# Turning keys, values and normed outputs of the prompt off TensorE: 32x32 blocks on VectorE and a round trip through DRAM, with the projections in another order

## The chip, the cores and the metric

One core of a Trainium2 chip runs the whole kernel. The metric is the device time of one execution in microseconds; of the kernel before it is the median of three runs, 1311.06 us.

## The reference, cut to what matters

One layer of a hybrid decoder over 1024 prompt tokens and 64 sample tokens (8 sequences of 8), model width 1024, all in float32. A combined projection gives queries, keys, values and gates for four retention heads and four mLSTM heads of width 128. Each head runs chunk by chunk (128 tokens), here for retention:

```python
def step(S, inp):
    qc, kc, vc = inp
    scores = jnp.einsum('bhnd,bhmd->bhnm', qc, kc) * dmat[None]
    out = (jnp.einsum('bhnm,bhmv->bhnv', scores, vc)
           + jnp.einsum('bhnd,bhdv->bhnv', qc, S) * xi[None, :, :, None])
    S_new = (S * chunk_decay[None, :, None, None]
             + jnp.einsum('bhmd,bhmv->bhdv', kc * zeta[None, :, :, None], vc))
    return S_new, out
...
ret_y = head_groupnorm(ret_out, ret_g) * jax.nn.silu(g_r)
...
ml_y = head_groupnorm(ml_out, ml_g) * jax.nn.sigmoid(o_m)
mix = jnp.concatenate([ret_y, ml_y], axis=-1).astype(x.dtype) @ w_out
```

The mLSTM heads do the same with data-dependent weights and a normaliser. After the mix come a residual, and a feed-forward layer with a short convolution. The state update contracts over tokens, the scores over the head's width, and the output projection over the width again; so keys and values are needed with features on the partitions and with tokens on the partitions, and the normed output has to be turned back.

## The kernel before, in words

Activations lie with features on the 128 partitions and tokens along the free axis, T = 1088 of them (1024 prompt, 64 sample), in four blocks b of 272 columns. `proj` computes one 128-wide piece of a projection: for each block `dense` issues 24 products (8 slices of the contraction, three terms of a split into high and low parts, line 160), 96 per projection; then an evacuation writes the block to a tile of tag `tok` (five of them): `evac_copy` by ScalarE for values, `evac_rot` (rotary) or `evac_norm` by VectorE for queries and keys. Two weight pieces are staged ahead by SP (`stage_w`, line 132) and split by ScalarE (line 144) and VectorE (line 146). `psA` has two PSUM banks, `psB` six.

`mix_head` runs for four retention heads (r0 to r3) and four mLSTM heads (m0 to m3). It projects queries, keys, values in this order (values of r0 and r1 come at the very start, as a pair). Then it goes through the chunks in pairs, [0,1] to [6,7], and the sample chunk [8]. `front` turns keys and values of a pair by TensorE into the PSUM bank `x_` (lines 632 and 633; `ident` is the identity), from which VectorE makes `kz` (keys times decay, line 636 or 640) and ScalarE `vt` (values times the norm of the token, line 644), computes the scores (line 666) and weighs them into `pt`. `pair_of` computes the state update (line 774) and the output (lines 779 and 781), evacuates the output to an `on` tile (three of them) and takes its statistics. `finish`, once for chunks 0 to 3, once for 4 to 7 and once for the sample, normalises `on` (line 707), turns it by TensorE (line 710) and scales it into the output tile `yT` (line 716 by VectorE for retention heads, where `yT` holds the gate already; line 718 by ScalarE for mLSTM heads). `finish` is held back: `finish_previous(b, row)` calls it within the next head's projections, with its transposes behind block b's products and its first VectorE operation behind an evacuation.

Order within an engine is set by a scheduler that simulates a timeline; `tc.issue_after` adds edges by hand. So the next head's first projection fills TensorE between the products of a head's chunks. Meanwhile GpSimd computes sums of feed-forward weights (`weight_sums`, line 823), a background stream of loads, subtractions and stores, first in the tile `wq`, later in `tab`, where the rotary tables were. They are read back in the feed-forward layer.

Of the kernel before, what the change touches and what calls it, by code (L numbers as in the profile page):

```python
# [16 lines left out]
P = 128  # L17
# [75 lines left out]
def hybrid_layer_kernel(ctx: ExitStack, tc: tile.TileContext, a: dict, o: dict):  # L93
# [166 lines left out]
    def tok(name, rows=P, dt=F32):  # L260
        return tokp.tile([P, T], dt, tag="tok", name=name)[:rows, :]
# [26 lines left out]
    wv = [tuple(wp.tile([P, D], F32R, tag="w" + part, name=f"w{part[0]}_in{i}") for part in ("hi", "lo")) for i in first]  # L288
    split_piece = lambda n, *after: split_to(*(t[:, pieces[n]] for t in (staged[0], *wv[0])), nc.vector, *after)
    split_piece(0)  # L290
    sums = [m2.tile([P, NB, 129], F32, tag=t, bufs=1, name=f"sums_{t}").rearrange("p s v -> p (s v)") for t in ("vx", "sb")]
    sqs = [tok(f"sq{i}").rearrange("p (k n) -> p k n", k=4) for i in range(2)]
    for b in range(5):
        if b % 2 == 0 and b < 4:
            h.append(quadrants("h", b // 2))
        if b < 4:
            gain_split(xs[b], V_PREMIX, h[b // 2], b)
        if b == 0:
            split_to(staged[1], *wv[1])
            continue  # L300
        nts.append(sums[(b - 1) // 3][:, (b - 1) % 3 * Q:((b - 1) % 3 + 1) * Q])
        last["sums"] = square_sum(xs[b - 1], nts[-1], sqs, nc.gpsimd if b == 4 else nc.vector)
# [22 lines left out]
        return out  # L325

    def spread_tile(name):
        return m2.tile([P, NB * 129], F32, tag="vx", bufs=1, name=name)

    rbd = dr.tile([1, T], F32, name="rbd")  # L330

# [36 lines left out]
        nc.scalar.activation(ig, ig, AF.Identity, bias=vec[0:NH, V_BG + 1:V_BG + 2])  # L368

    def gate_consts():  # L370
        xst = m2.tile([P, X_N], F32, tag="vx", bufs=1, name="xst")
        nc.sync.dma_start(xst, a["cx"])
        nc.vector.tensor_copy(upb, xst[:, X_UP:X_UP + P])
        for t in vts:
            nc.gpsimd.memset(t[:, :, P:P + 1], 1.0)
        nc.vector.tensor_copy(negsb, xst[:, X_NEGS:X_NEGS + P])
# [82 lines left out]


    yT = []

    def proj(*jobs, mid=None, done=None, banks=lambda i, b: psA, pair=False):

# [91 lines left out]
    def mix_head(hd, ml):  # L556
# [3 lines left out]
        if hid == 0:  # L560
            vs = [tok(f"v_r{i}") for i in range(2)]
            proj(*((i, evac_copy(t), w) for i, t, w in zip(first, vs, wv)),
                 banks=alternate, pair=True)
            early.extend(vs)
        v = early.pop(0) if early else tok(f"v_{nm}")
        q, k = tok(f"q_{nm}"), tok(f"k_{nm}")
        if ml:
            ub = ub_tile(f"ub{hd}")
            row = urows[hd:hd + 1, :]
            nc.sync.dma_start(ub, bass.AP(row.tensor, row.offset, [[0, P], [1, UB]]))  # L570
            proj((16 + hd, evac_norm(q, 1.0), split_w(staged.pop(), f"in{16 + hd}")))
            row = last["row", 3]
            proj((20 + hd, evac_norm(k, SCALE)), banks=alternate)
            finish_previous(2, row)
            proj((24 + hd, evac_copy(v)))
            finish_previous(1, last["row", 3])
            finish_previous(2, last["row", 3])
        else:
            eq, ek = evac_rot(q, f"q{nm}"), evac_rot(k, f"k{nm}")
            if hd == 0:  # L580
                proj((0, eq, split_to(stage_w(a["wi"][0], "in0"), *first_q)), mid=pre_norm, banks=lambda i, b: psB)
                here["wq"] = mp.tile([P, 2, 2, 2 * P], F32, tag="wq", name="wq")
                proj((NH, ek))
            else:
                proj((hd, eq))
                row = last["row", 3]
                proj((NH + hd, ek), banks=alternate)
                finish_previous(2, row)
                if hd == 1:
                    finish_previous(3, last["row", 1])  # L590
                    finish_previous(3, last["row", 2])
            if hd == 0:
                token_norms()
            if hd > 1:
                proj((2 * NH + hd, evac_copy(v)))
                finish_previous(1, last["row", 3])
                finish_previous(2, last["row", 3])
            if hd == 0:
                gate_proj()
                gate_consts()  # L600
                for _ in range(5):
                    next(rows)
                for i in range(NH):
                    proj((12 + i, early_gate(i)), banks=alternate)
                    next(rows)
                    next(wsums)
                log_exp_tables(last["sigmoid"])
                next(rows)

        if hid >= NH - 1:  # L610
            j = 12 + hid + 1 if hid + 1 < 2 * NH else 28
            staged.append(stage_w(a["wi"][j], f"in{j}"))
        sb = m2.tile([P, NB, 129], F32, tag="sb", bufs=1, name=f"sb_{nm}")
        nc.sync.dma_start(sb[:, :, :P], a["sc" if ml else "sr"][hd].rearrange("p (s v) -> p s v", s=NB))
# [6 lines left out]
        def front(cs):  # L621

            c0, L = cs[0], len(cs)
            nmc = f"{nm}{c0}"
            px = bank(psB, 512, f"x_{nmc}").rearrange("p (j i n) -> p j i n", j=2, i=2)
            if c0 < 8:
                kc, vc = ([chunk(t, c) for c in cs] for t in (k, v))
            else:
                own.append(spread_tile(f"sp_{nm}"))
                kc, vc = ([spread_copy(t, own[0][:, i * P:(i + 1) * P])] for i, t in enumerate((k, v)))  # L630
            for i, c in enumerate(cs):
                nc.tensor.transpose(px[:, 0, i, :], kc[i], ident)
                nc.tensor.transpose(px[:, 1, i, :], vc[i], ident)
            kz = m2.tile([P, 2, P], F32, tag="kz", name=f"kz_{nmc}")
            if ml:
                nc.vector.tensor_tensor(kz[:, :L], px[:, 0, :L, :],
                                        cols[:, c0:c0 + L, NH + hd].unsqueeze(2).broadcast_to([P, L, P]), ALU.mult)
            else:
                zc = C_ZE + hd + (0 if c0 < 8 else NH)
                nc.vector.tensor_scalar(kz[:, :L], px[:, 0, :L, :], rc(zc, 1), None, ALU.mult)  # L640
            vt = vts[0]
            vts.append(vts.pop(0))
            for i, c in enumerate(cs):
                nc.scalar.activation(vt[:, i, :P], px[:, 1, i, :], AF.Copy, scale=rcol[:, c:c + 1])
            qs = None
            if ml:
                wt, qs = (here["wq"][:, turns["wq"] % 2, i].rearrange("p (i n) -> p i n", i=2) for i in range(2))
# [35 lines left out]
        def finish(on, mv, c0, L, name, after=None, row=None):  # L683

            sh = [P, L]
            small = lambda tag: m2.tile([P, 4], F32, tag=tag, name=f"{tag}_{name}")[:, :L]
            vv, A = small("vv"), small("A")
            if ml:
                den, rd = small("den"), small("rd")
                dd = on[:, :L, P]  # L690
                with tc.issue_after(row.ins) if row else nullcontext():
                    nc.vector.scalar_tensor_tensor(den, dd, -1.0, dd, ALU.mult, ALU.max)
# [12 lines left out]
            ps = bank(psB, L * P, f"yt_{name}")  # L705
            for i in range(L):
                nc.vector.scalar_tensor_tensor(on[:, i, :P], on[:, i, :P], mv[:, i, 0:1],
                                               A[:, i:i + 1].broadcast_to([P, P]), ALU.subtract, ALU.mult)
                with tc.issue_after(after.ins) if after else nullcontext():
                    nc.tensor.transpose(ps[:, i * P:(i + 1) * P], on[:, i, :P], ident)  # L710
            y = yT[hid // 2][:, hid % 2, c0 * CH:c0 * CH + L * P if c0 < 8 else T]
            if c0 == 8:
                ps, y = spread(ps)[:, :, LEAD:], spread(y)
            gain = vec[:, V_HEAD + hid:V_HEAD + hid + 1]
            if hid in EARLY:
                nc.vector.scalar_tensor_tensor(y, ps, gain, y, ALU.mult, ALU.mult)
            else:
                nc.scalar.activation(y, ps, AF.Copy, scale=gain)
# [837 lines left out]
```

## Time and profile before

| | |
|---|---|
| median of 3 runs | 1311.06 us (1310.99 to 1311.78) |
| profiled execution, its own time | 1311.53 us |
| its span | 1309.7 us |
| TensorE busy | 1296.0 us, 99%, 10501 products |
| VectorE, ScalarE, GpSimd busy | 998.3, 600.0, 430.8 us |
| heads: first scores of r0, first scores of m0, start of the output projection | 110.80, 291.81, 495.09 us |
| output projection, feed-forward layer | from 495.09 us to the end |
| transfers | 194.46 MB, 148 GB/s in the mean |

Spans of products overlap since products are pipelined; what one takes from TensorE is the distance between starts. A row of a group gives line, engine, operation, names of output and inputs, shapes and count, then busy time and mean duration in ns, then idle time before it. A row of one line or tile gives durations as minimum/median/maximum. Rows by stretch give busy time of each engine with the number of instructions, the granted clock of TensorE, the busy share of the 16 transfer engines and GB/s. A row of transfers gives size and time to landing; a row of a queue gives packets, MB and the share of 16 engines.

### The profile page before, as it was taken

How to read it: one execution, taken by the hardware profiler on the slowest of the kernel's cores; microseconds unless marked ns; L12 is line 12 of the kernel's file. 1: busy time of each engine (PE TensorE's matmuls, PEld its weight loads, DVE VectorE, ACT ScalarE, POOL GpSimd, SP SyncE). 2: the span in 40 equal slices, each digit the busy share in tenths (PEclk: the TensorE clock that was granted, in tenths of full speed). 3: DMA queues.
4: the chain of work that ended last, by engine and by line, in shares of the span. 5: the costliest groups of instructions: out<-in, count | busy, mean ns of one | idle time of the engine just before them, and what ended most of it. 6: DMA issues, size and time to landing. Idle time of an engine off the chain costs nothing.

```text
span 1309.7 us, 26782 instructions
## 1 busy us (share of the span) xinstructions
PE 1296.0 (99%) x10501; PEld 1285.9 (98%) x10501; DVE 998.3 (76%) x2002; ACT 600.0 (46%) x1144; POOL 430.8 (33%) x564
## 2 busy tenths in 40 slices
PE   9999999999999999999999999999999999999996
PEld 9999999999999999999999999999999999999996
DVE  7774766657767655678999878787787888897678
ACT  7544433323433346455744434343443455543563
POOL 0354341758882000001334321222222214593002
PEclk9999999999999999999999999999999999999998
DMA  7344443567783124233144433444334469533363
GB/s 262 109 139 150 148 147 116 181 193 236 239 267 123 51 66 152 69 103 134 53 153 163 150 120 120 149 138 144 115 125 156 132 207 311 175 95 95 95 222 137
DMA packets 90784, 194.46 MB, mean 148 GB/s; under 512 B 13849, under 2 KB 39065, under 8 KB 90146
## 3 DMA queue, kind: packets, MB, share of 16 engines
q1 hardware_dynamic: 78210, 150.30, 34.4%
q0 software_dynamic: 12160, 41.95, 9.7%
q8 instruction: 82, 1.34, 0.4%
q10 hardware_dynamic: 288, 0.50, 0.1%
q14 instruction: 44, 0.36, 0.1%
HBM read 136.21 MB, written 56.50 MB: 147 GB/s over the span
## 4 chain that ended last, share of the span: by engine, by line
PE 96%; DVE 2%; DMA 1%; ACT 1%; issue 0%; SPq 0%
PE in L160 30%; PE out L160 7%; PE up_S L1130 6%; PE up_S L1129 6%; PE up_S L1128 6%; PE dn L1355 5%; PE dn L1356 5%; PE dn L1357 5%; PE up_A L1129 5%; PE up_A L1128 5%; PE up_A L1130 5%; PE up_A L1180 1%; PE up_A L1179 1%; PE up_A L1178 1%; DVE facc L1432 1%; PE s_r L666 1%
## 5 line engine op out<-in xcount | busy, mean ns | idle before, releaser
L160 PE MATMUL in<-hh,wh_in 128*128 128x272 f32 x960 | 277.8, 292 | 0.8 <-ACT hh L227 0.8
L160 PE MATMUL in<-hh,wl_in 128*128 128x272 f32 x960 | 277.4, 291 | 0.2 <-DVE wl_in L146 0.2
L160 PE MATMUL in<-hl,wh_in 128*128 128x272 f32 x960 | 277.1, 291 | 0.0
L160 PEld LDWEIGHTS in<-hh,wh_in 128*128 128x128 f32 x960 | 180.1, 188 | 2.8 <-issue 1.4
L160 PEld LDWEIGHTS in<-hh,wl_in 128*128 128x128 f32 x960 | 180.3, 188 | 1.4 <-issue 1.0
L160 PEld LDWEIGHTS in<-hl,wh_in 128*128 128x128 f32 x960 | 179.8, 188 | 0.9 <-issue 0.7
L144 ACT ACTIVATE wh_up<-st_up 128x1024 fp32r<-128x1024 f32 x84 | 80.5, 960 | 168.8 <-PE up_S L1129 97.1
L146 DVE TENSOR_TENSOR wl_up<-st_up,wh_up 128x1024 fp32r<-128x1024 f32 x84 | 96.0, 1144 | 9.9 <-ACT wh_up L144 9.9
L1102 DVE TENSOR_TENSOR Uv<-Uv,up_S 128x272 f32<-128x272 f32 (+1 forms) x200 | 66.4, 374 | 45.5 <-PE up_S L1130 45.5
L1283 DVE TENSOR_TENSOR rb<-rb 128x544 fp32r<-128x544 f32 x78 | 75.6, 974 | 28.7 <-ACT rb L1282 28.1
L1304 POOL TENSOR_TENSOR wd<-wd 128x512 f32<-128x512 f32 x44 | 74.5, 1715 | 47.0 <-DMA wd<-in_wd 20.0
L1282 ACT ACTIVATE rb<-rb 128x544 fp32r<-128x544 f32 x78 | 50.7, 651 | 82.2 <-DMA rb<-bd 71.2
L823 POOL TENSOR_TENSOR tab<-tab 128x256 f32<-128x256 f32 x104 | 79.1, 771 | 11.9 <-DMA tab<-in_wu 7.4
L1163 POOL TENSOR_TENSOR act<-act 128x544 f32<-128x544 f32 x40 | 63.4, 1586 | 58.0 <-DMA bd<-act 36.2
L1093 POOL MEMSET Ug<- 128x2 f32 x22 | 2.2, 99 | 221.5 <-DMA xr<-in_x 100.2
L1143 DVE SCALAR_TENSOR_TENSOR c<-Uv,vec,c 128x1024 f32<-128x1024 f32 (+1 forms) x88 | 68.5, 783 | 8.5 <-ACT c L1141 8.5
L1143 DVE SCALAR_TENSOR_TENSOR c<-Ug,vec,c 128x1024 f32<-128x1024 f32 x88 | 69.1, 825 | 0.0
L823 POOL TENSOR_TENSOR wq<-wq 128x256 f32<-128x256 f32 x56 | 47.8, 863 | 45.8 <-DMA wq<-in_wu 43.6
L144 ACT ACTIVATE wh_in<-st_in 128x1024 fp32r<-128x1024 f32 (+2 forms) x31 | 31.9, 1028 | 57.0 <-PE in L160 56.1
L1141 ACT ACTIVATE c<-Ug,vec 128x1024 f32<-128x1024 f32 (+1 forms) x44 | 34.6, 834 | 45.5 <-DVE Ug L1106 43.9
L823 POOL DMA_DIRECT2D tab<-in_wu x52 | 36.8, 713 | 33.1 <-DVE k_r L500 21.7
L1130 PE MATMUL up_S<-T1h,wl_up 128*128 128x272 f32 x160 | 46.4, 290 | 0.0
(557 smaller groups left out, 4652.8 us busy)
## 6 DMA issues: line engine op xcount, KB each, us to landing
rb<-bd SPq DMA_DIRECT2D x76, 272.0 KB, 2.8
st_up<-sd SPq DMA_DIRECT2D x40, 512.0 KB, 3.9
bd<-act SPq DMA_DIRECT2D x33, 544.0 KB, 3.3
st_in<-in_wi SPq DMA_DIRECT2D x31, 512.0 KB, 3.8
tab<-in_wu POOLq DMA_DIRECT2D x52, 256.0 KB, 5.3
sd<-tab POOLq DMA_DIRECT2D x26, 512.0 KB, 3.6
st_up<-in_wu SPq DMA_DIRECT2D x24, 512.0 KB, 3.2
wd<-in_wd SPq DMA_DIRECT2D x44, 256.0 KB, 5.1
```

The source lines that it names most:

```text
L144: act = nc.scalar.activation(hi, x, AF.Copy)
L146: last["split"] = act, eng.tensor_tensor(lo, x, hi.bitcast(F32), ALU.subtract)
L160: last["product", b] = nc.tensor.matmul(ps, u[:, k * P:(k + 1) * P], x[b // 2][k // 4][v][:, k % 4, qcols(b)], start=k == term == 0, stop= ...
L823: last["sums"] = f(*args)
L1102: nc.vector.tensor_tensor(o_, o_ if x is None else c(x), c(ps), ALU.add)
L1128: nc.tensor.matmul(ps, wh[:, c], xh[:, k, n], start=k == 0, stop=False)
L1129: nc.tensor.matmul(ps, wh[:, c], xl[:, k, n], start=False, stop=False)
L1130: nc.tensor.matmul(ps, wl[:, c], xh[:, k, n], start=False, stop=k == 3)
L1143: last["conv"] = nc.vector.scalar_tensor_tensor(c, u(i), cw(i), c, ALU.mult, ALU.add)
L1283: nc.vector.tensor_tensor(lo, x, hi.bitcast(F32), ALU.subtract)
L1304: last[out] = nc.gpsimd.tensor_tensor(quad(p, out), quad(p, x), quad(p, y), op)
L1355: nc.tensor.matmul(t, wh[:, ms], ah, start=k == 0, stop=False)
```

## The change

For the prompt's eight chunks, TensorE no longer turns anything. `flip` takes a finished half of a projection (blocks 0 and 1, or 2 and 3: 512 columns), lets VectorE transpose its 32x32 blocks into the one tile of tag `flip`, which also orders the columns by block, and writes it to a tile in DRAM; after the second half four transfers read it back, each to 32 partitions, with runs of 128 elements. Values are read back into their own tile, keys into another (`kt`). `flip_rows` does the same for the normed output of four chunks. `flipped` is the view through which `kz`, `vt` and the final scale read. The sample chunk is turned by TensorE as before. Each `mix_head` projects keys, then values, then queries, and the held-back `finish` calls move with them: the first behind the values, the second behind the first block's row of the queries, the sample's behind the second. Retention heads get the gain by ScalarE in place and the gate by VectorE, instead of one VectorE operation. Two spread tiles (`sums_0`, and the tile of tag `vx`) change their place or size.

```diff
+    CH4 = 4 * P
+    def flip(dst, src, name):
+        bounce = dr.tile([2, P, CH4], F32, tag="bounce", bufs=4, name=f"bounce_{name}")
+        def f(b):
+            if b % 2 == 0:
+                return
+            d = m2.tile([P, CH4], F32, tag="flip", bufs=1, name=f"flip_{name}{b // 2}")
+            x = src[:, b // 2 * CH4:(b // 2 + 1) * CH4]
+            nc.vector.transpose(d.rearrange("p (j c b) -> p c j b", j=4, c=4), x.rearrange("p (c j a) -> p c j a", c=4, j=4))
+            nc.sync.dma_start(bounce[b // 2], d)
+            if b == 3:
+                rows_ = bounce.rearrange("h (i a) n -> a (h i) n", i=4)
+                for j in range(4):
+                    nc.sync.dma_start(dst[32 * j:32 * j + 32, :8 * P].rearrange("p (g n) -> p g n", g=8),
+                                      rows_[:, :, j * P:(j + 1) * P])
+        return f
+    def flip_rows(dst, x, name):
+        bounce = dr.tile([P, CH4], F32, tag="bounce_y", bufs=4, name=f"bounce_{name}")
+        d = m2.tile([P, CH4], F32, tag="flip", bufs=1, name=f"flip_{name}")
+        nc.vector.transpose(d.rearrange("p (j c b) -> p c j b", j=4, c=4), x)
+        nc.sync.dma_start(bounce, d)
+        rows_ = bounce.rearrange("(i a) n -> a i n", i=4)
+        for j in range(4):
+            nc.sync.dma_start(dst[32 * j:32 * j + 32].rearrange("p (g n) -> p g n", g=4), rows_[:, :, j * P:(j + 1) * P])
...
             proj(*((i, evac_copy(t), w) for i, t, w in zip(first, vs, wv)),
-                 banks=alternate, pair=True)
+                 banks=alternate, pair=True,
+                 done=lambda b, fs=[flip(t, t, f"v_r{i}") for i, t in enumerate(vs)]: [f(b) for f in fs])
...
+        kt = yT[hid // 2][:, hid % 2] if ml else ub_tile(f"kt_{nm}")
+        flip_k = flip(kt, k, f"k_{nm}")
         if ml:
...
-            proj((16 + hd, evac_norm(q, 1.0), split_w(staged.pop(), f"in{16 + hd}")))
+            proj((20 + hd, evac_norm(k, SCALE), split_w(staged.pop(), f"in{20 + hd}")), done=flip_k)
             row = last["row", 3]
-            proj((20 + hd, evac_norm(k, SCALE)), banks=alternate)
+            proj((24 + hd, evac_copy(v)), done=flip(v, v, f"v_{nm}"))
             finish_previous(2, row)
-            proj((24 + hd, evac_copy(v)))
-            finish_previous(1, last["row", 3])
-            finish_previous(2, last["row", 3])
+            proj((16 + hd, evac_norm(q, 1.0)), banks=alternate)
+            finish_previous(3, last["row", 0])
+            finish_previous(3, last["row", 1])
...
             if c0 < 8:
-                kc, vc = ([chunk(t, c) for c in cs] for t in (k, v))
+                kx, vx = flipped(kt, c0, L), flipped(v, c0, L)
+                kc = [chunk(k, c) for c in cs]
...
-            for i, c in enumerate(cs):
-                nc.tensor.transpose(px[:, 0, i, :], kc[i], ident)
-                nc.tensor.transpose(px[:, 1, i, :], vc[i], ident)
...
+                turned = on.rearrange("p i w -> p (i w)")[:, :CH4]
+                flip_rows(turned, on[:, :, :P].rearrange("p c (j a) -> p c j a", j=4), f"y_{name}")
+                ps, y = flipped(turned, 0, 4), y.rearrange("p (c i b) -> p c i b", c=4, i=4)
             gain = vec[:, V_HEAD + hid:V_HEAD + hid + 1]
-            if hid in EARLY:
+            if hid in EARLY and c0 < 8:
+                nc.scalar.activation(turned, turned, AF.Copy, scale=gain)
+                nc.vector.tensor_tensor(y, y, ps, ALU.mult)
+            elif hid in EARLY:
                 nc.vector.scalar_tensor_tensor(y, ps, gain, y, ALU.mult, ALU.mult)
             else:
                 nc.scalar.activation(y, ps, AF.Copy, scale=gain)
```

More of the change, by code (lines that the diff above doesn't have):

```diff
@@ L290, in hybrid_layer_kernel @@
     split_piece(0)
-    sums = [m2.tile([P, NB, 129], F32, tag=t, bufs=1, name=f"sums_{t}").rearrange("p s v -> p (s v)") for t in ("vx", "sb")]
     sqs = [tok(f"sq{i}").rearrange("p (k n) -> p k n", k=4) for i in range(2)]
+    sums = [tok("sums_0"), m2.tile([P, NB, 129], F32, tag="sb", bufs=1, name="sums_1").rearrange("p s v -> p (s v)")]
     for b in range(5):
@@ L327, in spread_tile @@
     def spread_tile(name):
-        return m2.tile([P, NB * 129], F32, tag="vx", bufs=1, name=name)
+        return m2.tile([P, 4 * 129], F32, tag="vx", bufs=1, name=name)
     rbd = dr.tile([1, T], F32, name="rbd")
@@ L370, in gate_consts @@
     def gate_consts():
-        xst = m2.tile([P, X_N], F32, tag="vx", bufs=1, name="xst")
+        xst = m2.tile([P, 4 * 129], F32, tag="vx", bufs=1, name="xst")[:, :X_N]
         nc.sync.dma_start(xst, a["cx"])
@@ L461, in hybrid_layer_kernel, with flipped @@
     yT = []
+    CH4 = 4 * P
[22 more added lines that the diff above has]
+            nc.sync.dma_start(dst[32 * j:32 * j + 32].rearrange("p (g n) -> p g n", g=4), rows_[:, :, j * P:(j + 1) * P])
+    def flipped(t, c, L):
+        c0 = c % 4
+        return t[:, c // 4 * CH4:(c // 4 + 1) * CH4].rearrange("p (i c b) -> p c i b", i=4, c=4)[:, c0:c0 + L]
     def proj(*jobs, mid=None, done=None, banks=lambda i, b: psA, pair=False):
@@ L582, in mix_head @@
                 here["wq"] = mp.tile([P, 2, 2, 2 * P], F32, tag="wq", name="wq")
-                proj((NH, ek))
+                proj((NH, ek), done=flip_k)
             else:
-                proj((hd, eq))
+                proj((NH + hd, ek), done=flip_k)
                 row = last["row", 3]
-                proj((NH + hd, ek), banks=alternate)
-                finish_previous(2, row)
                 if hd == 1:
+                    proj((hd, eq), banks=alternate)
+                    finish_previous(2, row)
+                    finish_previous(3, last["row", 0])
                     finish_previous(3, last["row", 1])
-                    finish_previous(3, last["row", 2])
             if hd == 0:
@@ L594, in mix_head @@
             if hd > 1:
-                proj((2 * NH + hd, evac_copy(v)))
-                finish_previous(1, last["row", 3])
-                finish_previous(2, last["row", 3])
+                proj((2 * NH + hd, evac_copy(v)), done=flip(v, v, f"v_{nm}"))
+                finish_previous(2, row)
+                proj((hd, eq), banks=alternate)
+                finish_previous(3, last["row", 0])
+                finish_previous(3, last["row", 1])
             if hd == 0:
@@ L610, in mix_head @@
         if hid >= NH - 1:
-            j = 12 + hid + 1 if hid + 1 < 2 * NH else 28
+            j = 16 + hid + 1 if hid + 1 < 2 * NH else 28
             staged.append(stage_w(a["wi"][j], f"in{j}"))
@@ L624, in front @@
             nmc = f"{nm}{c0}"
-            px = bank(psB, 512, f"x_{nmc}").rearrange("p (j i n) -> p j i n", j=2, i=2)
+            wide = lambda t: t.rearrange("p c (i b) -> p c i b", i=4)
             if c0 < 8:
-                kc, vc = ([chunk(t, c) for c in cs] for t in (k, v))
+                kx, vx = flipped(kt, c0, L), flipped(v, c0, L)
+                kc = [chunk(k, c) for c in cs]
             else:
@@ L630, in front @@
                 kc, vc = ([spread_copy(t, own[0][:, i * P:(i + 1) * P])] for i, t in enumerate((k, v)))
-            for i, c in enumerate(cs):
-                nc.tensor.transpose(px[:, 0, i, :], kc[i], ident)
-                nc.tensor.transpose(px[:, 1, i, :], vc[i], ident)
+                px = bank(psB, 2 * P, f"x_{nmc}").rearrange("p (j n) -> p j n", j=2)
+                nc.tensor.transpose(px[:, 0, :], kc[0], ident)
+                nc.tensor.transpose(px[:, 1, :], vc[0], ident)
+                kx, vx = (wide(px[:, i:i + 1, :]) for i in range(2))
             kz = m2.tile([P, 2, P], F32, tag="kz", name=f"kz_{nmc}")
             if ml:
-                nc.vector.tensor_tensor(kz[:, :L], px[:, 0, :L, :],
-                                        cols[:, c0:c0 + L, NH + hd].unsqueeze(2).broadcast_to([P, L, P]), ALU.mult)
+                nc.vector.tensor_tensor(wide(kz[:, :L]), kx, cols[:, c0:c0 + L, NH + hd].unsqueeze(2).unsqueeze(3)
+                                        .broadcast_to([P, L, 4, 32]), ALU.mult)
             else:
                 zc = C_ZE + hd + (0 if c0 < 8 else NH)
-                nc.vector.tensor_scalar(kz[:, :L], px[:, 0, :L, :], rc(zc, 1), None, ALU.mult)
+                nc.vector.tensor_scalar(wide(kz[:, :L]), kx, rc(zc, 1), None, ALU.mult)
             vt = vts[0]
@@ L643, in front @@
             for i, c in enumerate(cs):
-                nc.scalar.activation(vt[:, i, :P], px[:, 1, i, :], AF.Copy, scale=rcol[:, c:c + 1])
+                nc.scalar.activation(vt[:, i, :P].rearrange("p (i b) -> p i b", i=4), vx[:, i], AF.Copy, scale=rcol[:, c:c + 1])
             qs = None
@@ L704, in finish @@
             nc.vector.tensor_tensor(A, A, rd, ALU.mult)
-            ps = bank(psB, L * P, f"yt_{name}")
             for i in range(L):
@@ L708, in finish @@
                                                A[:, i:i + 1].broadcast_to([P, P]), ALU.subtract, ALU.mult)
-                with tc.issue_after(after.ins) if after else nullcontext():
-                    nc.tensor.transpose(ps[:, i * P:(i + 1) * P], on[:, i, :P], ident)
             y = yT[hid // 2][:, hid % 2, c0 * CH:c0 * CH + L * P if c0 < 8 else T]
             if c0 == 8:
+                ps = bank(psB, P, f"yt_{name}")
+                with tc.issue_after(after.ins) if after else nullcontext():
+                    nc.tensor.transpose(ps, on[:, 0, :P], ident)
                 ps, y = spread(ps)[:, :, LEAD:], spread(y)
+            else:
+                turned = on.rearrange("p i w -> p (i w)")[:, :CH4]
+                flip_rows(turned, on[:, :, :P].rearrange("p c (j a) -> p c j a", j=4), f"y_{name}")
+                ps, y = flipped(turned, 0, 4), y.rearrange("p (c i b) -> p c i b", c=4, i=4)
             gain = vec[:, V_HEAD + hid:V_HEAD + hid + 1]
-            if hid in EARLY:
+            if hid in EARLY and c0 < 8:
+                nc.scalar.activation(turned, turned, AF.Copy, scale=gain)
+                nc.vector.tensor_tensor(y, y, ps, ALU.mult)
+            elif hid in EARLY:
                 nc.vector.scalar_tensor_tensor(y, ps, gain, y, ALU.mult, ALU.mult)
```

## The prediction

> **What bounds the kernel now.** I read the page first, then the busy time by stretch, then the chain of waits through the heads.
>
> ```profile
> PE 1296.0 (99%) x10501; PEld 1285.9 (98%) x10501; DVE 998.3 (76%) x2002; ACT 600.0 (46%) x1144; POOL 430.8 (33%) x564
> ...
> PE 96%; DVE 2%; DMA 1%; ACT 1%; issue 0%; SPq 0%
> ```
> ```profile
> core 0: us, PE busy (x) PEld busy (x) DVE busy (x) ACT busy (x) POOL busy (x), PEclk, DMA share, GB/s
> 0.00:65.00 65.00, 62.89 (x506) 59.75 (x506) 49.46 (x102) 43.01 (x84) 10.67 (x21) 1.00 0.54 184
> 302.00:350.00 48.00, 48.00 (x408) 47.34 (x407) 33.51 (x105) 17.20 (x52) 40.60 (x57) 1.00 0.76 244
> ```
> ```profile
> 291.81 0.45 PE s_m L666 x4
> ...
> 295.54 0.45 PE u_m L774 x4
> ...
> 326.71 12.07 PE in L160 x96
> 339.76 0.45 PE s_m L666 x4
> ```
>
> TensorE is the chain: 96% of the way back from the end is PE, and it is never idle in the head stage. One mLSTM head takes 339.76 - 291.81 = 47.95 us; a whole projection (96 products) is 12.07 us of it. So an instruction taken off PE there is time saved, as long as PE finds other work when a turned tile isn't there. The clock granted is 1.00 in all these stretches, so no throttle changes the price of a product.
>
> **The change, part by part.**
>
> *1. Transposes leave PE.* Of every head, 8 of k, 8 of v and 8 of the normed output go; the ninth (sample) chunk keeps its three.
>
> ```profile
> L633 PE MATMUL x_m<-cst,v_m 128*128 128x128 f32 x32 | 7.9, 273 | 0.0
> L633 PE MATMUL x_r<-cst,v_r 128*128 128x128 f32 x32 | 7.9, 273 | 0.0
> L632 PE MATMUL x_r<-cst,k_r 128*128 128x128 f32 x32 | 7.9, 273 | 0.0
> L632 PE MATMUL x_m<-cst,k_m 128*128 128x128 f32 x32 | 7.9, 272 | 0.0
> ```
> ```profile
> L710 PE MATMUL yt_r<-cst,on_r x32: 270/272/273, 146.1 to 291.0; 128*128 128x128 f32 x32
> L710 PE MATMUL yt_m<-cst,on_m x32: 270/272/273, 326.1 to 470.6; 128*128 128x128 f32 x32
> ```
> ```profile
> 110.36 0.27 PE L632 MATMUL x_r<-cst,k_r 128*128 128x128 f32 x1
> ...
> 110.80 0.61 PE L666 MATMUL s_r<-q_r,k_r 128*128 128x128 f32 x4
> ```
>
> The listed 272 ns overlap; what a transpose takes from PE is its distance to the next start, (110.80 - 110.36) / 4 = 0.11 us. 6 x 32 = 192 transposes x 0.111 = **21.3 us**, 2.66 per head. That is the whole gain: nothing else leaves PE.
>
> *2. VectorE gains six block transposes per head* (two 128x512 halves of k, two of v, two of y), 48 in all. No block transpose is in this trace. The nearest rows are VectorE's 128x512 multiply and, for what a neighbour can do to an instruction that reads SBUF, the spread of the normalisation:
>
> ```profile
> L716 DVE SCALAR_TENSOR_TENSOR yT<-yt_r,vec,yT x8: 742/751/751, 147.0 to 291.3; 128x512 f32<-128x512 f32 x8
> L718 ACT ACTIVATE yT<-yt_m,vec x8: 671/672/679, 327.3 to 471.4; 128x512 f32<-128x512 f32 x8
> ```
> ```profile
> L707 DVE SCALAR_TENSOR_TENSOR on_m<-on_m,mv_m,A_m x32: 338/348/903, 318.8 to 459.8; 128x128 f32<-128x128 f32 x32
> ```
>
> I take 0.75 us (same columns); the high end is double, 1.5, below L707's worst stretch of 903/348. The low end is ScalarE's 0.67. Per head 6 x 0.75 = 4.5 us: VectorE goes from 33.51 us of 48 to 38.0 of 45.3, 84%; with 1.5 it is 42.5, still under PE. So as an average it is hidden behind PE. kz and vt now read SBUF instead of PSUM at the same shapes: taken as nothing. For retention heads ScalarE does an extra 128x512 scale, 2 x 0.67 us per head on an engine busy 17.20 us of 48: hidden.
>
> The Trainium skill, "VectorE: DVE Perf Modes", sections The three transpose paths and Rules for kernel authors, speaks against the change: VectorE turns only 32x32 blocks, and a 128x128 transpose belongs on TensorE when PSUM will do as a destination. It gives 311 ns for 128x128 in bf16; four make 1.24 us, an estimate from that page, and 6 x 1.24 = 7.4 us per head instead of 4.5. The sum would be the same, since 33.51 + 7.4 is still below 45.3. The rows show TensorE as the scarce engine; the rule does not ask which one is. What it could still turn around is the third rival.
>
> *3. The round trip.* A half of k or v is written in one transfer (256 KB), the whole read back in four (128 KB each, 512 B runs); y the same per four chunks. That is 22 more issues per head on SP's queue. Rows of nearest kind:
>
> ```profile
> sb_r<-in_sr SPq DMA_DIRECT2D x4, 512.0 KB, 4.1
> out_ss<-sb_r SPq DMA_DIRECT2D x4, 512.0 KB, 3.5
> sb_m<-in_sc SPq DMA_DIRECT2D x4, 512.0 KB, 6.1
> ```
> ```profile
> 258.76 0.34 SPq L807 DMA_DIRECT2D out_sp<-S_r  x1
> ```
>
> From the last product of v: evacuation and block transpose 0.4 + 0.75, write 3.5 (that row is twice the bytes, so a high end), four issues 4 x 0.34 = 1.4, last read 4.1 to 6.1: **10 to 12 us**. What covers it is the reordering: v is now projected before q, so a projection of 12.07 us lies between, and the first product that needs vt (u_m) starts 3.7 us after s_m (295.54 - 291.81). Slack 4 to 6 us; for k another 12. For v of heads 0 and 1 some 70 us. I cost it at nothing; without that cover each us late is a us of PE. SP is in order: 22 x 0.34 = 7.5 us per head fits, but each read waits for its write (up to 3.5 us) with the weight loads behind it in the same queue: at most 6 such waits, 21 us of a head's 45, for three loads that are each asked for one projection ahead. Nothing again; late weights are the first thing to look at if that fails.
>
> *4. The transfer engines.* 3 x 512 KB each way per head: 3072 packets of 512 B and 1.57 MB of writes.
>
> ```profile
> q1 hardware_dynamic: 3552, 2.17, 24.1%
> ```
> ```profile
> q0 software_dynamic: 1511, 5.23, 55.0%
> q1 hardware_dynamic: 3552, 2.70, 28.9%
> ```
>
> The first row (stretch 405 to 435) makes 0.241 x 16 x 30 us / 3552 = 33 ns per packet of 0.6 KB, 18.8 bytes per ns. So 3072 x 33 ns + 1.57 MB / 18.8 = 101 + 84 us over 16 engines: 11.6 us, a share of 0.25 of a 45-us head. In heads m0 and m1, where GpSimd's weight sums run (the second pair, 309 to 339), the mean is 0.76 already: about 1.0. GpSimd's sums get slower there and end later:
>
> ```profile
> 402.83 0.74 POOL L823 DMA_DIRECT2D sd<-tab  x1 [0.30 <-POOL tab L823]
> ```
>
> that is their last transfer, with two heads to go, and the feed-forward layer begins to read them after 620, so that costs nothing. The flips' latencies there are what I doubt: sb_m's 6.1 against sb_r's 4.1 is what such load did to one load, so 1 to 3 us more per round trip, inside the slack of v.
>
> *5. The output's second flip is the tightest.* It starts from the row of q's first quarter, so 9 us before the chunks begin. From the start of the divisions to the last normalised chunk took 374.57 to 381.62, 7 us:
>
> ```profile
> 352.87 0.37 ACT L677 ACTIVATE on_m<-o_m 128x258 f32<-128x258 f32 x1
> ```
> ```profile
> 374.57 0.16 DVE L692 SCALAR_TENSOR_TENSOR den_m<-on_m 128x4 f32<-128x4 f32 x1
> ...
> 380.48 1.14 DVE L707 SCALAR_TENSOR_TENSOR on_m<-on_m,mv_m,A_m 128x128 f32<-128x128 f32 x4
> ```
>
> Then 0.75 + 3.5 + 1.4 + 4 to 6 us: back some 8 to 10 us into the chunks, while the same `on` buffer (three of them) is wanted for the third pair, 13.1 us into them (352.87 - 339.76). ScalarE's final scale waits for that read at the head of its queue, with vt and the exponentials behind it, and PE behind these. Bounds per head: 0 (no less, since PE has no idle time there to win) to 2.7 (one read 3 us late, seen by PE almost whole). No stall of this kind is in the trace; I take 0.5, nearest to the zero idle PE shows in 302 to 350: 8 x 0.5 = 4.
>
> *6. The first stretch.* Values of heads 0 and 1 are turned between 20 and 40 us: four transposes on VectorE (3.0 us, busy 49.46 of 65), and the one turn buffer makes the second wait for a write, up to 3.5 us, with operand splits and the first evacuations behind it. PE idles only 2.1 us there. Bounds 0 (nothing here is taken off PE) to 6.5; I take 1.5, low because two of the four fall behind the operand splits:
>
> ```profile
> 26.87 1.32 DVE L228 SCALAR_TENSOR_TENSOR hl<-x,vec,hh 128x272 fp32r<-128x272 f32 x3
> ```
>
> (the last splits end at 28.1 us).
>
> **Sum.** The profiled execution took 1311.53 us (span 1309.7 plus 1.8 around it), 0.47 above the median of 1311.06. Against it: -21.3 + 4 + 1.5 = -15.8, 1295.7; against the median 1295.3. I say **1295.5**.
>
> **Rivals.**
>
> First, *a part is given back*: the same mechanism as in 5, at 1.3 to 2.3 us per head, mostly in m0 and m1 and r3 under full transfer engines. 8 x 1.8 + 1.5 = 16: 1306. For it: 0.76 + 0.25. Against: m2 and m3 have 0.24 of that share left over.
>
> Second, *no change*: PE finds no filler. With 16 transposes fewer in its stretch, a head's chunks last as long as VectorE's chain does, and PE idles what it saved. 1311. Against it, the next head's products in the 18 us of a head's chunks:
>
> ```profile
> 291.00:309.00 18.00, 9.12 (x57) 7.55 (x57) 1.00 0.62 211
> ```
>
> 57 x 12.07 / 96 = 7.2 us; 1.8 more leaves 3 of the projection's 12.07.
>
> Third, *slower: VectorE's queue becomes the bound in the chunks.*
>
> ```profile
> 291.00:309.00 18.00, 18.00 (x169) 17.36 (x167) 15.63 (x52) 10.81 (x33) 16.28 (x23) 1.00 0.62 211
> ```
>
> It is busy 15.63 of 18 us there. The next head's k is now the filler, so its first half is turned within these 18 us, and the previous output's second turn too: 15.63 + 2 x 0.75 = 17.1 against PE's 18 - 16 x 0.111 = 16.2; with 1.5 each, 18.6. And one turn buffer: where two turns come within the 3.5 us of a write, the queue stands up to 3 us with evacuations and kz behind it. It decides from 2.66 us of PE per head; at 3.5 it is 8 x 0.84 + 1.5 = +8: 1319. The page of the Trainium skill named in part 2 points this way. Against it: the idle waits of VectorE in the other 30 us of a head can take work from the chunks.
>
> **How the numbers follow.** A measurement of this kernel can tell about 0.2%, 2.6 us, from no change: faster is under 1308.4, slower over 1313.7. The forecast has 0.54 (1289 to 1301: full saving, or 1.2 us lost per head), the first rival 0.17, the second 0.08, the third 0.21. Faster 0.71, same 0.08, slower 0.21. The low end is full saving, 1311.1 - 21.3 = 1289.8, and 0.1% for the scatter of runs; the high end takes in the first two rivals and the start of the third, 1315. The forecast's own range is 1289 to 1301.
>
> **What would show it.** Right: PE's matmul count down by 192, to 10309; no k and v operands of chunks 0 to 7 in the transposes; a head's period 45.3 to 46; block transposes of 0.7 to 0.8 us; PE idle in 65 to 480 under 6 us. Wrong: PE waiting on kz, vt or evacuations in each head for over 2.7 us; a block transpose over 1.5 us; VectorE or ScalarE long idle on a read of the bounce, above all ahead of the final scale; first products late before 65 us.

## The result, and the profile after

The changed kernel takes **1344.74 us** (median; 1339.98 to 1354.22), the kernel before in the same runs 1311.24. The ratio is **1.0264 [1.0207, 1.032]**: slower by 33.5 us, where 15.6 less were forecast and the range ended at 1315. The profiled execution took 1339.98 us (span 1338.2), 4.8 under the median: it shows 28.5 us of the loss (1338.2 - 1309.7).

First the busy totals of the changed kernel's page, and the shares of the chain that ended last:

```profile
PE 1288.4 (96%) x10309; PEld 1274.6 (95%) x10309; DVE 1023.2 (76%) x2050; ACT 609.6 (46%) x1152; POOL 434.0 (32%) x564
...
PE 79%; DMA 10%; DVE 5%; SPq 2%; issue 1%; ACT 1%; POOL 1%; DVEq 0%; ACTq 0%
```

PE (TensorE) lost its 192 transposes (10501 to 10309), yet PE's share of the chain fell from 96% to 79%, and transfers and VectorE came in. Then the heads, 110 to 495 us, kernel before and kernel after:

```profile
110.00:495.00 385.00, 385.00 (x3255) 379.77 (x3254) 257.76 (x818) 146.20 (x403) 180.25 (x245) 1.00 0.49 159
```
```profile
65.00:110.00 45.00, 45.00 (x368) 44.46 (x361) 30.62 (x48) 19.17 (x28) 21.95 (x25) 1.00 0.46 148
495.00:525.00 30.00, 30.00 (x241) 30.00 (x241) 19.63 (x34) 14.82 (x27) 0.00 (x0) 1.00 0.26 75
110.00:495.00 385.00, 348.71 (x2835) 339.69 (x2834) 258.82 (x828) 140.75 (x382) 183.34 (x246) 0.96 0.70 212
```

PE stands idle for 36.3 us of these 385, and its clock falls to 0.96 on average; around them nothing is lost. The out projection starts at 523.3 us instead of 494.9 (first product of each in TensorE's own records; the 495.09 of the table further up is the chain's): 28.4 of the 28.5. VectorE has gained the turns, but in these 385 us it is no busier than before (258.82 to 257.76). Over the whole of the heads, from 110 us to the out projection, its share is 67% in both kernels, so no engine became the bound. PE's idle times over the heads, by what ended them:

```profile
PE in L160 <- DVE q_r L534: 7.9, 3, 4.0
PE yt_m1s L753 <- DVE on_m1s L747: 7.6, 1, 7.6
PE yt_m0s L753 <- DVE qx L771: 6.5, 1, 6.5
PE in L160 <- DVE q_m L524: 5.6, 2, 3.3
PE yt_r3s L753 <- DVE on_r3s L747: 3.6, 1, 3.6
```

PE never waits long for a turned tile. It waits for query evacuations and for the previous head's normed sample outputs (`on_m1s` and its like; the row with `qx` is that of `on_m0s`, done 0.15 us earlier), which TensorE turns as before. What these stand behind is in the other engines' waits (VectorE, then ScalarE, over the heads; us in total, times, longest):

```profile
DVE kz_m L677 <- DMA yT<-bounce_k_m: 34.2, 4, 10.9
DVE kz_r L681 <- DMA kt_r<-bounce_k_r: 12.9, 4, 4.1
...
DVE flip_v_r L473 <- DMA bounce_k_r<-flip_k_r: 8.0, 2, 4.2
DVE flip_y_r L486 <- DMA bounce_y_r<-flip_y_r: 6.8, 2, 4.0
```
```profile
ACT wq L695 <- DVE wq L700: 35.0, 4, 13.5
...
ACT on_r L761 <- DMA on_r<-bounce_y_r: 18.7, 7, 5.5
```

The longest of them, step by step, in VectorE's and SP's timelines while head m2's keys and values are prepared (start, duration, instruction, idle time before it and its releaser):

```profile
384.21 0.70 DVE L473 STREAM_TRANSPOSE flip_k_m<-k_m 128x512 f32<-128x512 f32 x1
...
393.51 0.71 DVE L473 STREAM_TRANSPOSE flip_v_m<-v_m 128x512 f32<-128x512 f32 x1 [2.37 <-DMA bounce_k_m<-flip_k_m]
405.15 1.35 DVE L677 TENSOR_TENSOR kz_m<-yT,cols 128x256 f32<-128x256 f32 x2 [10.93 <-DMA yT<-bounce_k_m]
406.43 0.70 DVE L473 STREAM_TRANSPOSE flip_v_m<-v_m 128x512 f32<-128x512 f32 x1
...
408.16 0.42 DVE L524 SCALAR_TENSOR_TENSOR q_m<-in,rb 128x272 f32<-128x272 f32 x1
```
```profile
384.94 0.32 SPq L474 DMA_DIRECT2D bounce_k_m<-flip_k_m  x1
...
393.43 5.62 SPq L478 DMA_DIRECT2D yT<-bounce_k_m  x4
399.09 8.40 SPq L474 DMA_DIRECT2D bounce_v_m<-flip_v_m  x2
```

The keys' last half is turned at 384.2. Its 256 KB write is over only at 393.4, 8.5 us after the issue at 384.94; the four reads are issued from 393.4 to 399.1, and the keys are back at 405.15: 21 us for a round trip that the prediction put at 10 to 12. Meanwhile kz, the first instruction that reads them, stands at the head of VectorE's queue for 10.9 us. PE asks for kz only after the scores at 418.4. But behind kz in the queue are the values' second turn and the query evacuation q_m, whose PSUM bank PE needs. On SP, the write of the values' first half (turned at 393.5) stands behind the keys' four reads, which stand behind the keys' write. PE stops for 2.3 us, goes on for 1.9, and stops again:

```profile
408.73 0.36 PE L160 MATMUL in<-hh,wh_in 128*128 128x272 f32 x1 [2.30 <-DVE q_m L524]
...
418.14 0.44 PE L753 MATMUL yt_m1s<-cst,on_m1s 128*128 128x128 f32 x1 [7.55 <-DVE on_m1s L747]
```
```profile
410.00:418.00 8.00, 0.58 (x5) 0.36 (x3) 7.37 (x26) 1.23 (x6) 7.23 (x10) 0.79 0.87 259
418.00:420.00 2.00, 1.86 (x9) 1.89 (x9) 0.34 (x1) 0.00 (x0) 0.48 (x1) 0.50 1.06 355
422.00:424.00 2.00, 2.00 (x11) 2.00 (x10) 0.83 (x1) 1.33 (x3) 1.70 (x3) 0.50 0.76 245
426.00:430.00 4.00, 4.00 (x37) 4.00 (x36) 4.00 (x16) 3.07 (x11) 2.28 (x3) 1.00 0.85 267
```

In the second stop VectorE is busy 7.37 of 8 us: it works off what piled up behind kz. And PE pays twice, since it comes back at half clock (0.50 in both stretches after the stop, 1.00 from 426).

The account: 28.4 us later in spite of 21.3 saved is 49.7 lost. 36.3 are PE's idle time. The lower clock makes about 10.4 more (in steps of 1 us from 110 to 523, PE's busy time times what the granted clock lacks to 1.00). The last 3 stay open.

### The profile page after: what moved, and what is told of

The parts are those of the page before. It is cut to its first block, busy times and chain, and to the rows that moved or that the text cites. A ratio compares the mean times of both kernels' runs of the same rounds, so it can differ in the third digit from the quotient of the medians.

```text
span 1338.2 us, 26770 instructions
## 1 busy us (share of the span) xinstructions
PE 1288.4 (96%) x10309; PEld 1274.6 (95%) x10309; DVE 1023.2 (76%) x2050; ACT 609.6 (46%) x1152; POOL 434.0 (32%) x564
## 4 chain that ended last, share of the span: by engine, by line
PE 79%; DMA 10%; DVE 5%; SPq 2%; issue 1%; ACT 1%; POOL 1%; DVEq 0%; ACTq 0%
PE in L160 17%; PE out L160 7%; PE up_S L1178 6%; PE up_S L1177 6%; PE up_S L1176 6%; PE dn L1403 5%; PE dn L1404 5%; PE dn L1405 5%; PE up_A L1177 5%; PE up_A L1176 4%; PE up_A L1178 4%; DMA bounce_v_m<-flip_v_m 2%; DMA v_m<-bounce_v_m 1%; DMA bounce_k_r<-flip_k_r 1%; PE up_A L1228 1%
## 5 line engine op out<-in xcount | busy, mean ns | idle before, releaser
L1331 DVE TENSOR_TENSOR rb<-rb 128x544 fp32r<-128x544 f32 x78 | 77.4, 997 | 28.5 <-ACT rb L1330 28.3
L1178 PE MATMUL up_S<-B3h,wl_up 128*128 128x272 f32 x160 | 46.3, 290 | 0.0
```

Of the source, the lines that this page charges most:

```text
L1178: nc.tensor.matmul(ps, wl[:, c], xh[:, k, n], start=False, stop=k == 3)
L1331: nc.vector.tensor_tensor(lo, x, hi.bitcast(F32), ALU.subtract)
```

## The experiments

**The theory.** The block transposes and the transfers' bytes are not the loss by themselves. Each engine runs its queue in order, and the new order puts the readers of the bounce (kz on VectorE; vt and the output's final scale on ScalarE) ahead of work that PE needs sooner. A late read stands there, and the queue behind it too. The load beside it decides how late. The expectations call this theory A. **Rivals**: the block transposes slow VectorE down; the new order of projections costs the time; the transfers' load alone does, wherever the readers stand (B in the expectations); the one turn buffer does (C).

Medians in us, ratios with their 95% intervals; "out" is the start of the out projection in the profiled execution (494.9 before, 523.3 after). The kernel before stood at 1311.2 to 1311.4 in all these runs.

| run | median | ratio to before | out |
|---|---|---|---|
| e4_order_only | 1311.22 | 0.9999 [0.9989, 1.0009] | |
| e9_turn_only | 1291.07 | 0.9847 [0.9833, 0.9862] | 475.3 |
| e1_pin_kz | 1340.89 | 1.0219 [1.0199, 1.0239] | |
| e3_own_turn | 1346.52 | 1.0262 [1.0237, 1.0288] | |
| e2_no_sums | 1306.04 | 0.9952 [0.9935, 0.9969] | |
| e5_before_no_sums | 1311.05 | 0.9997 [0.9988, 1.0007] | |
| e6_no_sums_pin | 1302.93 | 0.9932 [0.9916, 0.9949] | |
| e10_kv_only | 1341.99 | 1.0235 [1.02, 1.027] | |
| e8_y_only | 1339.34 | 1.021 [1.019, 1.023] | 522.2 |
| e11_y_late | 1305.94 | 0.9959 [0.9943, 0.9975] | 487.3 |
| e12_keys_first | 1304.35 | 0.9947 [0.9934, 0.996] | 486.7 |
| e13_keys_y_late | 1303.05 | 0.9931 [0.9918, 0.9944] | 486.7 |

**e4: the new order alone**, on the kernel before, with TensorE's transposes.

```diff
-            proj((16 + hd, evac_norm(q, 1.0), split_w(...)))
+            proj((20 + hd, evac_norm(k, SCALE), split_w(...)))
...
+            proj((16 + hd, evac_norm(q, 1.0)), banks=alternate)
```

> The kernel before, with nothing but the new order: projections keys, values, queries, and the held-back finishes at their new places; everything is turned by TensorE as before. If the order alone costs (rotary tables freed later for GpSimd, finishes later), 1315 or more; theories A, B and C all expect the time of before within 3 us, 1308 to 1314.

1311.22 against 1311.29: the order costs nothing. That rival is out.

**e9: all 48 turns, no transfers.**

```diff
-            nc.sync.dma_start(bounce[b // 2], d)
-            if b == 3:
+            if False:
...
-                turned = on.rearrange("p i w -> p (i w)")[:, :CH4]
-                flip_rows(...)
+                turned = on[:, :, :P]
+                flip_rows(...)
```

> The changed kernel with all 48 block transposes on VectorE, but without the transfers: kz, vt and the final scale read the unturned tiles. That leaves out the second half of every transposition. If VectorE's and ScalarE's added work were a cost (third rival of the prediction by way of the work itself), 1300 or more; theories A, B and C, for all of which the transfers are the cause, expect the full saving of TensorE, 1289 to 1294.

1291.07, 20.1 under before: the whole saving but 1.2 us. Heads of e9, and one group of its turns:

```profile
110.00:495.00 385.00, 383.45 (x3217) 377.77 (x3217) 296.68 (x879) 170.95 (x431) 189.47 (x249) 1.00 0.54 171
```
```profile
L473 DVE STREAM_TRANSPOSE flip_k_m<-k_m x8: 697/700/712, 246.1 to 394.4; 128x512 f32<-128x512 f32 x8
```

VectorE carries them at 0.70 us each and is busy 296.68 of 385, with PE idle only 1.55. The transposes are not the cause; the round trip is.

**e1, e3: two single repairs.** e1 puts every kz behind the evacuation of the query's last row. e3 gives the normed output of the m heads its own turn buffer.

```diff
+            with tc.issue_after(last["row", 3].ins):
                 nc.vector.tensor_tensor(wide(kz[:, :L]), kx, ...)
```
```diff
-        d = m2.tile([P, CH4], F32, tag="flip", bufs=1, name=f"flip_{name}")
+        d = m2.tile([P, CH4], F32, tag="flip", bufs=1, name=f"flip_{name}") if own is None else own
...
-                flip_rows(turned, ..., f"y_{name}")
+                flip_rows(turned, ..., f"y_{name}", y if ml else None)
```

> The changed kernel, with one edge more: every kz (the product that reads the turned keys) may start on VectorE only after the evacuation of the last projection's fourth block. Theory A (place in the queue): the loss is VectorE standing at kz for the read-back of the keys (45 us of waiting in 110 to 525, up to 10.9 at once) with the queries' evacuations and the second turn of the values behind it; then this edge takes most of that wait away and 20 us or more of the 28.5 us of span come back, to below 1322. Theory B (transfers too slow under GpSimd's stream): the read-back is late in itself, the wait moves to values and vt, under 10 us come back. Theory C (one turn buffer): under 10 us come back, since the turns still wait for writes (30 us of waits).

> The changed kernel, with the normed output of the mLSTM heads turned into its own place in the output tile (which is written later anyway) instead of the one turn buffer; keys and values alone share that buffer then. Theory C: in m0 to m3 and the tail the turns' waits for a write (about 10 of 30 us) go, and 5 to 10 us come back. Theory A: 3 us or less, since what holds VectorE is kz.

Neither repairs it. e3 is where the changed kernel was, which rules the shared turn buffer out for the m heads' outputs only. e1 is about 4 us lower, with intervals that overlap, where theory A expected 20 or more: so kz alone is not what holds VectorE. The wait moves, as VectorE's rows of e1 show:

```profile
DVE flip_v_m L473 <- DMA bounce_v_m<-flip_v_m: 39.7, 4, 14.8
...
DVE flip_v_r L473 <- DMA bounce_v_r<-flip_v_r: 17.1, 2, 9.0
```

With kz out of the way, the values' second turn stands for the one turn buffer, which is free only when the first half's write has landed. So pinning one reader moves the head of the line to the next one that waits for a transfer.

**e2, e5, e6: the load.** GpSimd's weight sums and their transfers left out, from the changed kernel (e2), from the one before (e5), and from e1 (e6); the feed-forward layer then reads plain weights of the same size.

```diff
-        yield from stretch(0, 13, [own], 0)
-        yield from stretch(13, 18, [free[0], free[1], own], 2)
-        yield from stretch(18, len(parts), free, 2)
+        for _ in parts:
+            yield
```

> The changed kernel without GpSimd's sums of the feed-forward weights in the head stage: their loads, subtractions and stores are left out, and the feed-forward layer reads plain weights of the same size instead. Theory B: with the engines free (share 0.92 in 254 to 302 would fall to about 0.4) the round trips shorten by 3 us or more and 20 us or more come back. Theory A: VectorE still stands at kz, because the order is as before the first query evacuation; read-backs shorten by 2 to 4 us in r3 to m2 only, so 5 to 15 us come back, and m3, which had no stream beside it, keeps its 7.7 us wait. Theory C: 5 us or less.

> Control: the kernel before without GpSimd's sums (left out as in the run without sums). All theories: TensorE is never idle in the head stage either way, so the time of before within 3 us (1308 to 1314). If it is much faster, the 38 us between the changed kernel and the changed kernel without sums are not the round trip's alone.

> The changed kernel without GpSimd's sums, and with every kz behind the last evacuation on VectorE. Theory B (the stream beside it is the whole cause): the run without sums gave 1306, and the pin adds nothing. Theory A+C (what is left, 16 us over the full saving at 1290, is VectorE standing: 39 us of waits at kz): with the pin alone the second turn still waits for the first half's write, which stands behind the keys' read-backs in SP's queue; 3 to 8 us come back, to 1298 to 1303.

e2 is about 39 us below the changed kernel, which is what B expected (20 or more) and not A (5 to 15); e5 is where before was. The sums alone cost nothing, then, and next to the round trips they decide between loss and gain. But the wait for kz shrinks only from 34.2 to 29.2 us, and e2 is only 5.3 under before, a quarter of the 21.3; its longest wait of this kind:

```profile
DVE kz_m L677 <- DMA yT<-bounce_k_m: 29.2, 4, 7.6
```

Pinning kz on top of it (e6) may bring 3 us more (the intervals overlap). The sums are an amplifier, and not by the transfers alone. In the kernel before they also lengthen VectorE's instructions: without them VectorE is busy 234.00 us in the heads (e5, below) instead of 257.76, with as many instructions (819 and 818); one normalisation of the m heads takes 349 ns in the mean instead of 453. e2 takes away both, the transfers' load and this, and doesn't tell them apart.

```profile
110.00:495.00 385.00, 385.00 (x3257) 379.77 (x3256) 234.00 (x819) 146.75 (x404) 0.00 (x0) 1.00 0.21 63
```

Whether the readers' place counts by itself is the next question.

**e10 and e8: the two halves.** e10 turns only keys and values by the round trip, e8 only the normed output; TensorE does the rest.

```diff
+                    nc.tensor.transpose(ps[:, i * P:(i + 1) * P], on[:, i, :P], ident)
...
-                flip_rows(turned, on[:, :, :P].rearrange("p c (j a) -> p c j a", j=4), f"y_{name}")
```
```diff
-            proj((20 + hd, evac_norm(k, SCALE), split_w(...)), done=flip_k)
+            proj((20 + hd, evac_norm(k, SCALE), split_w(...)))
...
-            proj((24 + hd, evac_copy(v)), done=flip(v, v, f"v_{nm}"))
+            proj((24 + hd, evac_copy(v)))
```

> The changed kernel with the normed output turned by TensorE again; keys and values go the new way. 14.2 us leave TensorE. The run with the output alone lost 35 us against its own saving. If that loss is the output's (ScalarE standing at the final scale), and the keys' and values' round trips add little, about 1305; if keys and values lose as much by themselves (VectorE standing at kz, values' second turn behind it, 45 us of waits), 1325 or more; the two losses then overlap in the changed kernel, which is only 5 us slower than the output alone.

> Only the normed output is turned by VectorE and a round trip; keys and values by TensorE, in the new order of projections. 64 transposes x 0.111 = 7.1 us leave TensorE. If the output's round trip costs nothing by itself (its turns and its read-backs then have the turn buffer, SP's queue and 2/3 of the new traffic to themselves): 1304 to 1306. If ScalarE's waits for its read-back (30 us in the changed kernel, 5.5 at once) reach TensorE by themselves: 1310 or more.

Each alone loses nearly all of it (+30.6 and +28.2 us). These are two losses that overlap, not two shares of one. In e10 VectorE stands at the m heads' kz for 34.4 us, as in the changed kernel. In e8 the standing queue is ScalarE's, and VectorE then waits for ScalarE (waits of e8, ScalarE and VectorE):

```profile
ACT yT L743 <- DMA on_m<-bounce_y_m: 49.4, 7, 13.6
...
ACT on_r L738 <- DMA on_r<-bounce_y_r: 32.3, 7, 7.6
```
```profile
DVE yT L739 <- ACT on_r L738: 28.1, 6, 7.3
DVE t_m L195 <- ACT t_m L194: 23.6, 6, 10.2
```

81.7 us of ScalarE's time go to the final scale's reads, 5.8 per wait. This is the mechanism of step 5 of the prediction.

**e11: the decisive one.** e8 with the same transfers; only the final scale is held back, to stand behind the next head's first vt (chunks 0 to 3) and behind an evacuation of its second pair (4 to 7).

```diff
+            def scale(after=None):
+                with tc.issue_after(after.ins) if after else nullcontext():
                     ...
+            if c0 < 8:
+                late.append(scale)
...
+        if late:
+            late.pop(0)(last["vt"])
...
+            if i == 1 and late:
+                late.pop(0)(last["on"])
```

> The output alone by round trip, as before, but its last step (ScalarE's scale, and VectorE's product with the gate) is held back: for chunks 0 to 3 behind the next head's first vt, for chunks 4 to 7 behind the evacuation of the next head's second pair. The transfers are the same. Theory A for ScalarE (it stands at the head of its queue for 81 us of read-backs, with weight splits, root of the variance and vt behind it): 25 us or more of the 28 come back, to 1304 to 1312. Theory B alone (the engines are full, whoever waits): the loss stays, 1330 or more.

33 us faster than e8, with a write that is slower if anything (transfers of e8, then of e11: KB each, median us to landing) and PE without an idle moment (heads of e11):

```profile
bounce_y_m<-flip_y_m SPq DMA_DIRECT2D x8, 256.0 KB, 5.5
```
```profile
bounce_y_m<-flip_y_m SPq DMA_DIRECT2D x8, 256.0 KB, 6.4
```
```profile
110.00:495.00 385.00, 385.00 (x3249) 379.77 (x3248) 281.42 (x842) 159.99 (x418) 189.00 (x245) 1.00 0.59 184
```

The rival "load, wherever the readers stand" falls here for the outputs: same bytes, same sums, later place, loss gone. 64 transposes are worth 64 x 0.111 = 7.1 us; the median got 5.5 of it.

**e12, e13: what can be kept.** e12 sends the keys of all heads and the values of r0 and r1, which have a projection or more between turn and reader, through the round trip with kz pinned, and leaves the rest to TensorE. e13 adds e11's outputs.

```diff
-            proj((24 + hd, evac_copy(v)), done=flip(v, v, f"v_{nm}"))
+            proj((24 + hd, evac_copy(v)))
...
+            with tc.issue_after(last["row", 3].ins):
                 nc.vector.tensor_tensor(wide(kz[:, :L]), kx, ...)
```

> Only round trips with long cover: the keys of all heads (24 us, two projections, before their first use), and the values of heads r0 and r1 (70 us); kz behind the last evacuation on VectorE. Values of the other heads and all outputs by TensorE. 80 transposes, 8.9 us, leave TensorE. If cover longer than the longest round trip seen (21 us, keys of m2) is what it takes: 1302 to 1304. If the transfers cost by their load on the engines (late weights, slower sums): 1308 or more.

> Both of the above together: keys, values of r0 and r1, and outputs with the held-back scale; 144 transposes, 16.0 us, leave TensorE. If cover is all that is needed, 1295 to 1300. If the two streams' transfers lengthen each other beyond their covers (two thirds of the changed kernel's new traffic), 1305 or more.

e12 gets 7.1 of 80 x 0.111 = 8.9 us, with keys that take as long to read as in the changed kernel (transfers of e12; 6.3 there) and one idle time of PE over the heads:

```profile
yT<-bounce_k_m SPq DMA_DIRECT2D x16, 128.0 KB, 6.2
```
```profile
PE in L160 <- DVE k_m L514: 0.3, 1, 0.3
```

e13 removes 144 transposes, 16.0 us, and gets 8.4: faster than before and after, but its interval overlaps e12's, and the out projection starts at the same 486.7. Its further 7.1 us went into new waits (heads of e13, and its longest idle times of PE):

```profile
110.00:495.00 385.00, 379.66 (x3176) 373.49 (x3175) 281.23 (x855) 160.34 (x414) 186.03 (x245) 1.00 0.67 204
```
```profile
PE yt_m0s L761 <- DVE on_m0s L755: 2.3, 1, 2.3
PE yt_r0s L761 <- DVE on_r0s L755: 2.0, 1, 2.0
```

PE is idle 5.3 us. e13's 1303.05 lies between the two cases that it was to decide, so neither holds as it was put. But the run answers for the load once more: with three quarters of the new traffic (144 of 192 transposes) and a transfer share of 0.67 in the heads, where the changed kernel has 0.70, PE stands for 5.3 us and not for 36.3. What stays untested are the values of heads r2 to m3, sent through memory with their readers held back. Not tried: a second turn buffer for keys and values, a longer cover for the late heads' values, and the whole change with every reader held back. How much of the 21.3 us could be kept at best is open.

## Why the prediction was wrong, point by point

- **Step 1 held.** 192 instructions fewer, and e9 shows 20.1 of the 21.3 us.
- **Step 2 held.** 0.70 us against 0.75, hidden behind PE. The rule weighed there (the Trainium skill, "VectorE: DVE Perf Modes", The three transpose paths and Rules for kernel authors) gave an estimate of 1.24 us; the trace has 0.70. Its advice to transpose on TensorE came out right here, by the round trip and not by the turn.
- **Step 3 failed, and this is the step that decided.** It compared the round trip with the time until PE needs the result, and costed it at nothing. The reader's place in its own engine's queue was not looked at: kz needs the keys only for the products after 418, but its turn on VectorE came at 394, and everything behind it waited. The 10 to 12 us were also 21 in the worst case, because one SP queue carries write, reads and the next write in order and the terms were added as if each were issued when ready. In its place the runs showed VectorE standing at kz for 34.2 us of the m heads, up to 10.9 at once, and PE idle for 36.3 us behind such waits. SP's waits had been priced only for the weight loads.
- **Step 4 was mis-sized.** Full transfer engines were foreseen (0.25 + 0.76; the profile has 0.90 to 0.92 in the three stretches below), at 1 to 3 us more per round trip. The writes of keys and values alone took 5.0 and 6.4 us in the m heads (medians; the output's 3.2), and those of the keys up to 8.5, against 3.5 taken as a high end. That end was the retention heads' state write, carried over to the m heads, whose load is another. The stretches (the second is the one shown of before, at 0.76 and PE 48.00):

```profile
254.00:302.00 48.00, 43.05 (x357) 41.57 (x355) 32.51 (x90) 13.17 (x39) 34.61 (x48) 1.00 0.92 269
302.00:350.00 48.00, 47.14 (x380) 46.11 (x381) 33.17 (x89) 15.17 (x41) 39.84 (x55) 0.96 0.91 279
350.00:398.00 48.00, 38.16 (x306) 37.10 (x306) 32.16 (x102) 17.92 (x51) 39.48 (x53) 0.89 0.90 273
```

- **Step 5 had the mechanism and not the size.** "At the head of its queue, with vt and the exponentials behind it" is what e8 shows. It was bounded at 2.7 us per head and taken at 0.5, "nearest to the zero idle PE shows"; idle time before the change says nothing of a wait that the change brings in. e8's 28.2 us over before and the 7.1 that its 64 transposes are worth make 35 us, 4.4 per head, nine times the price.
- **Step 6 was too dear.** The first head's scores start at 110.09 us, against 110.80 before; 0.44 of the difference is the four transposes that stood ahead of them. Nothing was lost there.
- **The rivals.** The third had the right sign and named the one turn buffer, but its main bound, VectorE busy in the chunks, was not it: in the 385 us of the heads VectorE was no busier than before, and in e9, where it carries the same turns and is busy 296.68 us, nothing of this is lost. Its 1319 is 26 us short. No case had two queues standing at once, nor PE's half clock after its longer stops. The sign of being wrong that did come, VectorE and ScalarE idle on reads of the bounce, was named.

## What to carry to other kernels

When a value is sent through memory, find its first reader's place in that engine's queue and list what stands behind it: the round trip should be over before that place comes, not before the moment the result is needed. Hold such readers back behind work that is needed sooner (e11: 33 us for a few lines), and when one is held back look at once for the next wait, since the repair of one (e1) only moved it. Take a transfer's latency from a stretch with the load that it will meet, with the queue's own order in the sum.

## What was not expected of the hardware

- **Half clock after a stop.** After the 7.55 us stop that ended at 418.14 the granted clock was 0.50 until about 424.8, 6.6 us later; after the 6.5 us stop that ended at 362.2 until about 366.8, 4.6 us; after the 3.6 us stop that ended at 302.3 until about 305.4, 3.1 us. The Trainium skill, "TensorE: Matmul & The Clock Gate", Part 1, says that TensorE drops to half clock after an idle window of about 3.4 us and needs about 3.4 us of sustained work to get back. The trace agrees on the drop and the half; two of these three ways back took longer, the one of 4.6 us with PE fed all the time.
- **One write, 2.0 to 8.5 us.** The same 256 KB write of the keys took between these in one execution, longest at 384.94, in a stretch where the transfer engines' share was 0.90 (350 to 398).
- **Queues in order.** VectorE and ScalarE did not pass a waiting instruction in the rows shown: up to 10.9 us at kz, and up to 13.6 at the final scale (e8). "PSUM — Partial Sum Buffer" of the Trainium skill, Engine vs sequencer instructions, states that these queues are strict FIFO; these rows agree.
